# Dilated attention on quadrants of the array: 64 queries by 192 keys in place of 128 by 256

## The chip, the cores and the metric

The kernel runs on one core of a Trainium2 chip. A core has a matrix engine (PE, with its weight loads shown as PEld), a vector engine (DVE), a scalar engine (ACT), GpSimd (POOL) and a queue engine (SP) that issues most of the DMAs here. The metric is the device time of one execution in microseconds; the median of several runs is compared.

## The reference

Two layers of a decoder trunk over 1024 positions of width 1024, all in float32. The first layer mixes by dilated sliding-window attention, the second by a gated linear recurrence; each is followed by a squared-ReLU MLP. Only the attention is touched here:

```python
DILATED_PATTERNS = ((128, 1), (512, 4), (2048, 16))      # (window, dilation)
proj = (x @ w_in).reshape(B, S, N_GROUPS, 3, ATTN_HEADS, ATTN_HEAD_DIM)
for g, (window, dilation) in enumerate(DILATED_PATTERNS):
    q, k = rotary(proj[:, :, g, 0], pos), rotary(proj[:, :, g, 1], pos)
    o, lse = dilated_window_attention(q, k, proj[:, :, g, 2], window, dilation)
...
s = jnp.einsum('znqhe,znkhe->znhqk', qb, kk).astype(F32) * (E ** -0.5)
dist = qi + blk - kj
in_band = (dist >= 0) & (dist <= blk)
p = jnp.exp(s - m)
l = jnp.sum(p, axis=-1, keepdims=True)
o = jnp.einsum('znqhk,znkhe->znqhe', (p / l).astype(v.dtype), vv)
```

There are 16 heads of width 64. Each query sees itself and the 128 keys before it (128/1, 512/4) in its residue class, or 64 positions of its class at dilation 16 (a class has only 64). So in a block of 128 queries, query number i needs the keys i to i + 128 of the 256 keys of its own and the previous block: a band of 129.

## The kernel before

Everything is kept transposed: 128 partitions are the two heads of a pair (64 rows each), the free axis is the 1024 positions, regrouped by residue class. The queries, keys and values of a pair and a dilation (a *unit*; 8 pairs by 3 dilations, in the order 16, 4, 1) come out of a projection that is made by `product` (L787 to L832): 252 steps of 12 matmuls of 128 x 512 (L797 to L799). The attention of a unit is cut into pieces (`pieces`, L533), and the loop over the 252 products (L895) puts one list of pieces behind each product by a table (`fill`, with the offsets `OFFS`, `ROPES`, `STATS`, `MIX`). In that loop the order of PE and of DVE is fixed as written (`in_order`, L873); ACT and SP are ordered by the scheduler. The last two units (pair 7, dilations 4 and 1) go behind the loop and are spread over the first rows of the output projection, in the single-block form that `tail` returns (L663), with nothing fixed on PE.

For dilations 1 and 4 (g = 0 and 1) a unit has 8 blocks of 128 queries. A block *has a predecessor* (`has_prev`, L536) if it isn't the first of its class: 7 of 8 at dilation 1, 4 of 8 at dilation 4.

- `vtrans` (L539): 8 transposes of 128 x 128 turn vT into vn (keys on partitions), and ACT copies it out of PSUM in two halves (L546). vT is not used any more after that, and its slot of the pool `up` (49 slots of 4 KB per partition, for weights, activations and most else) comes free.
- `qk` (L549): per block and head one matmul with the 64 rows of that head, 128 queries as weights and 256 keys (128 without a predecessor) as moving columns, into the two banks `sb` (one for each head). DVE adds the mask and takes the row minimum (L572), ACT the exponential and the sum (L575). The result lies in a tile p as [head 0 | head 1], 256 columns each.
- `ptr` (L622): transposes p by 128 columns: four a block with a predecessor, two without (two such blocks share a tile), and ACT copies them to pts (L631).
- `pv` (L633): per block two key blocks by two heads, each a matmul with 128 keys on the rows, 64 columns of vn as weights and 128 queries moving, into the half of the bank `o` that belongs to the head. After four blocks ACT copies `o` to og (L650, L653).

Dilation 16 (`qk16`, `ptr16`, `pv16`, L578 to L620) already works on 64 x 64 quadrants: rows by head, columns by class.

SP's queue issues in one order: x operands (L449), weights (L460), the four DMAs that swap halves for the rotary (rot, L527), the softmax statistics (ml, L704 and L707) and weights for mixing the dilations (frow, L743), and for the output projection wor, onr and z (L1000, L1013, L1051).

Of the kernel before, what the change touches and what calls it, by code (L numbers as in the profile page):

```python
# [9 lines left out]
F32 = mybir.dt.float32  # L10
# [3 lines left out]
ALU = mybir.AluOpType  # L14
AX = mybir.AxisListType

P = 128
# [3 lines left out]
HD = 64  # L21
# [48 lines left out]
def trunk_kernel(  # L70
# [286 lines left out]
    def attention(pre, hc):  # L357
# [136 lines left out]
                v = nc.vector  # L494
                v.tensor_sub(H[n][:, R], lows.pop(n), H[n][:, L].bitcast(F32))  # L495

        mask = cp.tile([P, 320], F32, name="mask")
        sel = cp.tile([P, NG * P], F32R, name="bsel")
        frow = U("frow", F32R)
        mdram = dp.tile([NPAIR, NG, 2, 2, S], F32, name="mdram")  # L500
# [32 lines left out]
        def pieces(pr, g, qT, kT, vT, og, sS, tail):  # L533
            st = {}

            def has_prev(b):  # L536
                return (g == 0 and b > 0) or (g == 1 and b % 2 == 1)

            def vtrans():  # L539
                vn = U("vn")  # L540
                for j in range(2):
                    pt = bank("pt", "vpt")
                    for i in range(4):
                        b = j * 4 + i
                        nc.tensor.transpose(pt[:, i * P:(i + 1) * P], vT[:, b * P:(b + 1) * P], ident)
                    act(vn[:, j * 512:(j + 1) * 512], pt, AF.Copy)  # L546
                st["vn"] = vn

            def qk(*tiles):  # L549
                sb = [bank("s", "s") for _ in range(2)]  # L550
                at, c0 = {}, 0
                for b in sum(tiles, ()):
                    prev = has_prev(b)
                    n = 256 if prev else 128
                    k0 = (b - 1 if prev else b) * P
                    at[b] = slice(c0, c0 + n)
                    c0 += n
                    for h in range(2):
                        nc.tensor.matmul(sb[h][:, at[b]], qT[h * HD:(h + 1) * HD, b * P:(b + 1) * P],  # L559
                                         kT[h * HD:(h + 1) * HD, k0:k0 + n], start=True, stop=True,  # L560
                                         skip_group_check=True)
                for tile_ in tiles:
                    whole = wp.tile([P, 512], F32, name="p", tag="p")
                    st["p", tile_] = whole
                    for i, b in enumerate(tile_):
                        prev = has_prev(b)
                        n = 256 if prev else 128
                        m = mask[:, 0:256] if prev else mask[:, 128:256]
                        p = [whole[:, (2 * i + h) * n:(2 * i + h + 1) * n] for h in range(2)]
                        for h in range(2):  # L570
                            nm = sS[:, 0, h, b:b + 1]
                            nc.vector.tensor_tensor_reduce(p[h], sb[h][:, at[b]], m, -0.125, 3.0e38,  # L572
                                                           op0=ALU.add, op1=ALU.min, accum_out=nm)
                        for h in range(2):
                            act(p[h], p[h], AF.Exp, bias=sS[:, 0, h, b:b + 1], scale=-1.0,  # L575
                                accum_out=sS[:, 1, h, b:b + 1])

            def qk16(j):  # L578
                sb = [bank("s", "s") for _ in range(2)]
                whole = wp.tile([P, 512], F32, name="p", tag="p")  # L580
                blocks = [(b, cl, slice((b % 4 * 2 + cl) * 64, (b % 4 * 2 + cl) * 64 + 64))
                          for b in range(4 * j, 4 * j + 4) for cl in range(2)]
                for b, cl, c in blocks:
                    q = slice(b * P + cl * 64, b * P + cl * 64 + 64)
                    for h in range(2):
                        r = slice(h * HD, (h + 1) * HD)
                        nc.tensor.matmul(sb[cl][(h ^ cl) * HD:(h ^ cl) * HD + HD, b % 4 * 64:b % 4 * 64 + 64],
                                         qT[r, q], kT[r, q], start=True, stop=True, skip_group_check=True)
                for b, cl, c in blocks:
                    nc.vector.tensor_tensor_reduce(whole[:, c], sb[cl][:, b % 4 * 64:b % 4 * 64 + 64],  # L590
                                                   mask[:, 256:320], -0.125, 3.0e38, op0=ALU.add, op1=ALU.min,
                                                   accum_out=sS[:, 0, cl, b:b + 1])
                for b, cl, c in blocks:
                    act(whole[:, c], whole[:, c], AF.Exp, bias=sS[:, 0, cl, b:b + 1], scale=-1.0,
                        accum_out=sS[:, 1, cl, b:b + 1])
                st["p", j] = whole
# [25 lines left out]
            def ptr(tile_):  # L622
                pt = bank("pt", "ppt")
                pts = wp.tile([P, 512], F32, name="pts", tag="pts", bufs=4)
                p = st.pop(("p", tile_))
                n = len(tile_) * 2 * (2 if has_prev(tile_[0]) else 1)
                for i in range(n):
                    nc.tensor.transpose(pt[:, i * P:(i + 1) * P], p[:, i * P:(i + 1) * P], ident)  # L628
                for i, b in enumerate(tile_):
                    st["pt", b] = pts[:, i * 256:]  # L630
                act(pts[:, :n * P], pt[:, :n * P], AF.Copy)  # L631

            def pv(b):  # L633
                if b % 4 == 0:
                    st["o"] = bank("o", "o")
                o = st["o"]
                pts = st.pop(("pt", b))
                nb = 2 if has_prev(b) else 1
                for i in range(nb):
                    kb = b - nb + 1 + i  # L640
                    for h in range(2):
                        nc.tensor.matmul(o[h * HD:(h + 1) * HD, (b % 4) * P:(b % 4 + 1) * P],
                                         st["vn"][:, kb * P + h * HD:kb * P + (h + 1) * HD],
                                         pts[:, (h * nb + i) * P:(h * nb + i + 1) * P],
                                         start=i == 0, stop=i == nb - 1, skip_group_check=True)
                if b % 4 == 3:
                    hb = b // 4
                    d = DIL[g]
                    if d == 1:
                        act(og[:, hb * 512:(hb + 1) * 512], o, AF.Copy)  # L650
                    else:
                        r = d // 2
                        act(og.rearrange("p (n r) -> p r n", r=d)[:, hb * r:(hb + 1) * r, :],  # L653
                            o.rearrange("p (r n) -> p r n", r=r), AF.Copy)

            def qks(*tiles):
                return [lambda: qk(*tiles)]

            def run(f, bs):
                return [lambda b=b: f(b) for b in bs]  # L660

            one = [(b,) for b in range(8)]
            if tail:  # L663
                return [
                    qks(*one[0:2]) + [vtrans],
                    qks(*one[2:4]) + run(ptr, one[0:2]),
                    run(pv, (0, 1)) + qks(*one[4:6]) + run(ptr, one[2:4]),
                    run(pv, (2, 3)) + qks(*one[6:8]) + run(ptr, one[4:6]),
                    run(pv, (4, 5)) + run(ptr, one[6:8]),
                    run(pv, (6, 7)),  # L670
                ]
            first, second = run(pv, range(4)), run(pv, range(4, 8))
            if g == 2:
                return [run(qk16, (0,)) + [vtrans], run(qk16, (1,)) + run(ptr16, (0,)), run(ptr16, (1,)),
                        [pv16], [], []]
# [1244 lines left out]
def _constants():  # L1920
    import numpy as np

    f = np.float32
    half = HD // 2
    inv = (f(10000.0) ** (-np.arange(half, dtype=f) * f(2.0 / HD))).astype(f)
    ang = inv[:, None] * np.arange(S, dtype=f)[None, :]
    c, s = np.cos(ang).astype(f), np.sin(ang).astype(f)
    cos_t = np.concatenate([c, c, c, c], 0)
    sin_t = np.concatenate([-s, s, -s, s], 0)
    qi = np.arange(P)[:, None]  # L1930
    kj = np.arange(P)[None, :]
    neg = f(-1.0e30)
    prev = np.where(kj >= qi, f(0), neg)
    own = np.where(kj <= qi, f(0), neg)
    pk = np.where(kj[:, :64] <= qi % 64, f(0), neg)
    masks = np.concatenate([prev, own, pk], 1).astype(f)
    cm = ((kj >= qi) & (kj // CH == qi // CH)).astype(f)
    cmask = np.tile(cm, (1, 4))
    sm = np.ones((P, S), f)
    sm[:, ::CH] = 0.0  # L1940
    rows = np.arange(P)[:, None]
    bsel = np.concatenate([((rows // 4 == g) & (rows % 2 == np.arange(P)[None, :] // HD)).astype(f)
                           for g in range(NG)], 1)
    return {"cos_t": cos_t, "sin_t": sin_t, "masks": masks, "cmask": cmask, "smask": sm, "bsel": bsel}
# [49 lines left out]
```

## Time and profile before

| | us |
|---|---|
| median of 3 runs | 2746.34 (2744.36 to 2746.37) |
| the profiled execution | 2742.7 |
| its span in the profile | 2740.9 |
| mean granted clock of PE, share of full | 0.998 |
| matmul records of scores, values and transposes at dilations 1 and 4 | 1808 (512, 864, 432) |

The page lists engines with their busy time and share, groups of instructions by line with "out<-in", shape, count, busy time and the mean in ns of one, and what the engine waited for before them. A shape like 64*128 ahead of an operand's is that of the array: rows by columns used. Rows of a timeline begin with the start and the time to the modelled end of the last instruction of the row, both in us. Rows of a table by stage give the stage, its length, then busy time and instructions in it for PE, PEld, DVE, ACT and POOL. Rows "A <- B: t, n, m" say that A waited for B for t us in total, n times, at most m us.

### The profile page before, as it was taken

The numbers are of one execution on the slowest core, as the hardware profiler recorded it, in microseconds if no ns is written. First come the engines' busy times: TensorE is split into PE (matmuls) and PEld (weight loads), VectorE is DVE, ScalarE is ACT, GpSimd is POOL, SyncE is SP. The second block draws the span as 40 slices with busy tenths as digits, with TensorE's granted clock in tenths as the row PEclk, the third lists the DMA queues.
The fourth block names the chain that finished last, engine by engine and source line by source line (L and its number), as shares of the span: only waits on it lengthen the run. The fifth ranks groups of instructions, "written<-read, shape, count | busy, mean of one in ns | idle before, by whom it ended". The sixth has DMA issues, their size and how long they took to land.

```text
span 2740.9 us, 41042 instructions
## 1 busy us (share of the span) xinstructions
PE 2714.7 (99%) x14760; PEld 2218.5 (81%) x14760; DVE 2069.9 (76%) x3876; ACT 1402.9 (51%) x3043; POOL 68.9 (3%) x46
## 2 busy tenths in 40 slices
PE   9999999999999999999999999999999999999998
PEld 7788888888788777888888888888888888888887
DVE  8868887787887779776696787566578886778687
ACT  5555555555555546444554345555542544445443
POOL 0000000000000002000000000011100100000000
PEclk9999999999999999999999999999999999999999
DMA  8767666767767324554675752010242464485653
GB/s 301 262 210 228 195 209 190 235 193 225 217 208 243 109 98 156 192 193 151 205 266 167 237 169 93 31 59 35 74 127 100 154 226 162 152 297 181 220 179 127
DMA packets 204299, 485.03 MB, mean 177 GB/s; under 512 B 29248, under 2 KB 43072, under 8 KB 204096
## 3 DMA queue, kind: packets, MB, share of 16 engines
q1 hardware_dynamic: 203328, 482.16, 53.2%
q8 instruction: 116, 1.90, 0.3%
q14 instruction: 87, 0.71, 0.1%
q10 hardware_dynamic: 768, 0.26, 0.0%
HBM read 362.66 MB, written 94.11 MB: 167 GB/s over the span
## 4 chain that ended last, share of the span: by engine, by line
PE 90%; DVE 7%; ACT 2%; issue 1%; DMA 1%; SPq 0%; POOL 0%; DVEq 0%; ACTq 0%; POOLq 0%
PE pmm L797 7%; PE pmm L799 7%; PE pmm L798 7%; PE pup L1319 7%; PE pup L1317 7%; PE pup L1318 7%; PE pdy L1471 4%; PE pdy L1468 4%; PE pdy L1472 4%; PE pdx L1471 3%; PE pdx L1472 3%; PE pdx L1468 3%; PE pmm L192 3%; PE pmm L194 3%; PE pmm L193 3%; PE ppt L628 2%
## 5 line engine op out<-in xcount | busy, mean ns | idle before, releaser
L797 PE MATMUL pmm<-xh,H 128*128 128x512 f32 x1008 | 403.7, 400 | 1.9 <-ACT H L487 1.9
L799 PE MATMUL pmm<-xh,H 128*128 128x512 f32 x1008 | 394.6, 391 | 1.7 <-DVE H L495 1.6
L798 PE MATMUL pmm<-xl,H 128*128 128x512 f32 x1008 | 393.9, 391 | 0.7 <-DVE xl L158 0.7
L799 PEld LDWEIGHTS pmm<-xh,H 128*128 128x128 f32 x1008 | 189.6, 188 | 44.1 <-DVE H L495 3.3
L797 PEld LDWEIGHTS pmm<-xh,H 128*128 128x128 f32 x1008 | 189.9, 188 | 40.8 <-ACT H L487 3.0
L798 PEld LDWEIGHTS pmm<-xl,H 128*128 128x128 f32 x1008 | 190.0, 189 | 38.1 <-DVE xl L158 1.5
L1468 PE MATMUL pdy<-dT,dS 128*128 128x512 f32 x512 | 199.2, 389 | 0.0
L1471 PE MATMUL pdy<-dT,dS 128*128 128x512 f32 x512 | 199.2, 389 | 0.0
L1472 PE MATMUL pdy<-dT,dS 128*128 128x512 f32 x512 | 199.2, 389 | 0.0
L575 ACT ACTIVATE p<-p,stats 128x256 f32<-128x256 f32 (+1 forms) x256 | 118.3, 465 | 72.8 <-DVE stats L572 72.1
L157 ACT ACTIVATE dS<-dr 128x512 fp32r<-128x512 f32 x192 | 119.3, 622 | 68.5 <-PE pdy L1472 35.5
L192 PE MATMUL pmm<-f0nh,wh 128*128 128x512 f32 x384 | 153.2, 399 | 0.0
L194 PE MATMUL pmm<-f0nh,wl 128*128 128x512 f32 x384 | 149.8, 390 | 0.0
L193 PE MATMUL pmm<-f0nl,wh 128*128 128x512 f32 x384 | 149.7, 390 | 0.0
L158 DVE TENSOR_TENSOR dS<-dr,dS 128x512 fp32r<-128x512 f32 x192 | 131.4, 685 | 9.2 <-ACT dS L157 9.2
L572 DVE CUSTOM_DVE_ANT_0 p<-s,mask 128x256 f32<-128x256 f32 (+1 forms) x256 | 82.7, 380 | 58.4 <-PE s L559 49.0
L157 ACT ACTIVATE dT<-hold 128x512 fp32r<-128x512 f32 x128 | 80.1, 626 | 80.7 <-DVE hold L1447 34.0
L1278 ACT ACTIVATE H<-wc 128x512 fp32r<-128x512 f32 x128 | 77.2, 625 | 77.2 <-DVE wc L1271 47.9
L1468 PEld LDWEIGHTS pdy<-dT,dS 128*128 128x128 f32 x512 | 96.1, 188 | 20.1
L1472 PEld LDWEIGHTS pdy<-dT,dS 128*128 128x128 f32 x512 | 96.1, 188 | 19.9
L1471 PEld LDWEIGHTS pdy<-dT,dS 128*128 128x128 f32 x512 | 96.1, 188 | 19.9
L487 ACT ACTIVATE H<-wc 128x512 fp32r<-128x512 f32 x108 | 66.6, 630 | 70.4 <-DVE wc L479 53.8
(424 smaller groups left out, 6860.4 us busy)
## 6 DMA issues: line engine op xcount, KB each, us to landing
xh<-xtd SPq DMA_DIRECT2D x110, 512.0 KB
xl<-xtd SPq DMA_DIRECT2D x110, 512.0 KB
dr<-hd SPq DMA_DIRECT2D x192, 256.0 KB
dr<-in_w_down_dram SPq DMA_DIRECT2D x128, 256.0 KB
rot<-e SPq DMA_DIRECT2D x192, 128.0 KB
wa<-in_w_up_dram SPq DMA_DIRECT2D x48, 512.0 KB
wb<-in_w_attn_dram SPq DMA_DIRECT2D x36, 512.0 KB
wa<-in_w_attn_dram SPq DMA_DIRECT2D x33, 512.0 KB
```

What stands on the lines that cost most here:

```text
L157: act(hi, raw, AF.Copy)
L192: nc.tensor.matmul(o, wh[:, k], xs.h(k), start=k == 0, stop=False)
L193: nc.tensor.matmul(o, wh[:, k], xs.l(k), start=False, stop=False)
L194: nc.tensor.matmul(o, wl[:, k], xs.h(k), start=False, stop=k == NK - 1)
L797: nc.tensor.matmul(o, wh, hi[k // 2][:, c], start=begin and k == 0, stop=False, skip_group_check=True)
L798: nc.tensor.matmul(o, wh, lo[k // 2][:, c], start=False, stop=False, skip_group_check=True)
L799: nc.tensor.matmul(o, wl, hi[k // 2][:, c], start=False, stop=end and k == 3, skip_group_check=True)
L1317: nc.tensor.matmul(o, wh, xf.h(b, k), start=begin and k == 0, stop=False, skip_group_check=True)
L1318: nc.tensor.matmul(o, wh, xf.l(b, k), start=False, stop=False, skip_group_check=True)
L1468: nc.tensor.matmul(o[q], h, T_[:, L], start=begin, stop=False, skip_group_check=True)
L1471: nc.tensor.matmul(o[q], h, T_[:, R], start=False, stop=False, skip_group_check=True)
L1472: nc.tensor.matmul(o[q], l, T_[:, L], start=False, stop=end, skip_group_check=True)
```

## The change

The 128 queries of a block with a predecessor are taken in two halves a = 0, 1 of 64. Half a needs the keys 64 a to 64 a + 191 of the 256, so 192 columns stand in p for each head, not 256. The scores become four matmuls (half by head), each on its own 64 x 64 quadrant; blocks without a predecessor are split the same way with 128 keys each. The tile p of a block is [head 0, 192 | head 1, 192] and has three transposes; the middle one holds the last 64 keys of head 0 on its upper 64 partitions and the first 64 of head 1 on its lower ones. Where the 128 keys on the partitions don't begin at a block, values are needed that are shifted by 64: three DMAs on SP write them from vn over vT, which lives on until the last value product. Per half and head there is now one product over 128 keys (`first`) and one over the other 64 (`rest_`), both with 64 moving columns. `pv` takes all blocks of a call together and makes all of `first` before all of `rest_`. The mask has a band for 192 columns.

```diff
-        mask = cp.tile([P, 320], F32, name="mask")
+        mask = cp.tile([P, 384], F32, name="mask")
...
                 st["vn"] = vn
+                if g < 2:
+                    nc.sync.dma_start(vT[0:HD, :], vn[HD:P, :])
+                    nc.sync.dma_start(vT[HD:P, 0:7 * P], vn[0:HD, P:])
+                    nc.sync.dma_start(vT[HD:P, 7 * P:], vn[0:HD, 0:P])
...
-                    n = 256 if prev else 128
-                    k0 = (b - 1 if prev else b) * P
+                    n = 192 if prev else 128
                     at[b] = slice(c0, c0 + n)
                     c0 += n
-                    for h in range(2):
-                        nc.tensor.matmul(sb[h][:, at[b]], qT[h * HD:(h + 1) * HD, b * P:(b + 1) * P],
-                                         kT[h * HD:(h + 1) * HD, k0:k0 + n], start=True, stop=True,
-                                         skip_group_check=True)
+                    for a in range(2):
+                        k0 = (b - 1) * P + a * 64 if prev else b * P
+                        for h in range(2):
+                            r = slice(h * HD, (h + 1) * HD)
+                            nc.tensor.matmul(sb[h][a * 64:a * 64 + 64, at[b]],
+                                             qT[r, b * P + a * 64:b * P + a * 64 + 64], kT[r, k0:k0 + n],
+                                             start=True, stop=True, skip_group_check=True)
...
-                n = len(tile_) * 2 * (2 if has_prev(tile_[0]) else 1)
+                n = 3 if has_prev(tile_[0]) else 2 * len(tile_)
...
-                for i in range(nb):
-                    kb = b - nb + 1 + i
-                    for h in range(2):
-                        nc.tensor.matmul(o[h * HD:(h + 1) * HD, (b % 4) * P:(b % 4 + 1) * P],
-                                         st["vn"][:, kb * P + h * HD:kb * P + (h + 1) * HD],
-                                         pts[:, (h * nb + i) * P:(h * nb + i + 1) * P],
-                                         start=i == 0, stop=i == nb - 1, skip_group_check=True)
+                vn = st["vn"], vT
+                first, rest_ = [], []
+                for b in bs:
+                    pts = st.pop(("pt", b))
+                    for a, h in ((a, h) for a in range(2) for h in range(2)):
+                        f = slice(h * HD, (h + 1) * HD)
...
+                        if not has_prev(b):
+                            if a == 0:
+                                first.append((o[f, b % 4 * P:(b % 4 + 1) * P], v(0, b), pts[:, h * P:(h + 1) * P]))
+                            continue
+                        to = o[f, b % 4 * P + a * 64:b % 4 * P + a * 64 + 64]
+                        whole = v(a, b - 1) if h == 0 else v(1 - a, b - 1 + a)
+                        part = v(a, b, f) if h == 0 else v(1 - a, b - 2 + a, f)
+                        first.append((to, whole, pts[:, h * 256 + a * 64:h * 256 + a * 64 + 64]))
+                        rest_.append((to, part, pts[f, P + a * 64:P + a * 64 + 64]))
+                for n, (to, w, m) in enumerate(first):
+                    nc.tensor.matmul(to, w, m, start=bs[0] % 4 == 0 and n < 2, stop=False, skip_group_check=True)
+                for to, w, m in rest_:
+                    nc.tensor.matmul(to, w, m, start=False, stop=True, skip_group_check=True)
...
-            first, second = run(pv, range(4)), run(pv, range(4, 8))
+            first, second = [lambda: pv(0, 1, 2, 3)], [lambda: pv(4, 5, 6, 7)]
...
+    band = np.arange(192)[None, :] - qi % 64
+    prev = np.where((band >= 0) & (band <= P), f(0), neg)
```

The function `v(shift, t, r)` picks 64 columns of a head from vn (shift 0) or from the shifted copy in vT (shift 1), block t modulo 8, rows r. In the tail, `pv` is called for two blocks at a time, as in `[lambda: pv(0, 1)]`.

More of the change, by code (lines that the diff above doesn't have):

```diff
@@ L566, in qk @@
                         prev = has_prev(b)
-                        n = 256 if prev else 128
-                        m = mask[:, 0:256] if prev else mask[:, 128:256]
+                        n = 192 if prev else 128
+                        m = mask[:, 0:192] if prev else mask[:, 192:320]
                         p = [whole[:, (2 * i + h) * n:(2 * i + h + 1) * n] for h in range(2)]
@@ L590, in qk16 @@
                     nc.vector.tensor_tensor_reduce(whole[:, c], sb[cl][:, b % 4 * 64:b % 4 * 64 + 64],
-                                                   mask[:, 256:320], -0.125, 3.0e38, op0=ALU.add, op1=ALU.min,
+                                                   mask[:, 320:384], -0.125, 3.0e38, op0=ALU.add, op1=ALU.min,
                                                    accum_out=sS[:, 0, cl, b:b + 1])
@@ L631, in ptr, with pv, v @@
                 act(pts[:, :n * P], pt[:, :n * P], AF.Copy)
-            def pv(b):
-                if b % 4 == 0:
+            def pv(*bs):
+                if bs[0] % 4 == 0:
                     st["o"] = bank("o", "o")
                 o = st["o"]
-                pts = st.pop(("pt", b))
-                nb = 2 if has_prev(b) else 1
-                for i in range(nb):
-                    kb = b - nb + 1 + i
-                    for h in range(2):
-                        nc.tensor.matmul(o[h * HD:(h + 1) * HD, (b % 4) * P:(b % 4 + 1) * P],
-                                         st["vn"][:, kb * P + h * HD:kb * P + (h + 1) * HD],
-                                         pts[:, (h * nb + i) * P:(h * nb + i + 1) * P],
-                                         start=i == 0, stop=i == nb - 1, skip_group_check=True)
+                vn = st["vn"], vT
[4 more added lines that the diff above has]
+                        f = slice(h * HD, (h + 1) * HD)
+                        def v(shift, t, r=slice(0, P)):
+                            return vn[shift][r, t % 8 * P + f.start:t % 8 * P + f.stop]
+                        if not has_prev(b):
[11 more added lines that the diff above has]
+                    nc.tensor.matmul(to, w, m, start=False, stop=True, skip_group_check=True)
+                b = bs[-1]
                 if b % 4 == 3:
@@ L666, in pieces @@
                     qks(*one[2:4]) + run(ptr, one[0:2]),
[L667 to L670, printed above, removed]
+                    [lambda: pv(0, 1)] + qks(*one[4:6]) + run(ptr, one[2:4]),
+                    [lambda: pv(2, 3)] + qks(*one[6:8]) + run(ptr, one[4:6]),
+                    [lambda: pv(4, 5)] + run(ptr, one[6:8]),
+                    [lambda: pv(6, 7)],
                 ]
-            first, second = run(pv, range(4)), run(pv, range(4, 8))
+            first, second = [lambda: pv(0, 1, 2, 3)], [lambda: pv(4, 5, 6, 7)]
             if g == 2:
@@ L1932, in _constants @@
     neg = f(-1.0e30)
-    prev = np.where(kj >= qi, f(0), neg)
     own = np.where(kj <= qi, f(0), neg)
+    band = np.arange(192)[None, :] - qi % 64
+    prev = np.where((band >= 0) & (band <= P), f(0), neg)
     pk = np.where(kj[:, :64] <= qi % 64, f(0), neg)
```

## The prediction

> **What bounds the kernel.** I read the page first, then who waits for whom on PE, then a table by stage, then the groups by line and shape.
>
> ```profile
> span 2740.9 us, 41042 instructions
> PE 2714.7 (99%) x14760; PEld 2218.5 (81%) x14760; DVE 2069.9 (76%) x3876; ACT 1402.9 (51%) x3043; POOL 68.9 (3%) x46
> PE pmm L205 <- DVE wol L158: 1.9, 2, 1.1
> 85.00:940.00 855.00, 851.71 (x5736) 688.16 (x5736) 674.69 (x1504) 479.60 (x1312) 0.96 (x1) 1.00 0.67 210
> 940.00:1060.00 120.00, 114.13 (x623) 86.92 (x622) 91.78 (x216) 68.39 (x193) 2.10 (x2) 1.00 0.32 111
> ```
>
> PE is busy 99% of the span, and its worst releaser (the view is sorted, this is its first row) costs 1.9 us; no DMA is among its releasers. The table's columns are PE, PEld, DVE, ACT, POOL, granted clock, DMA share, GB/s. In attention (85 to 940 us) PE works 851.71 of 855 us at full clock, DVE 674.69, ACT 479.60, the DMA engines 0.67. So a microsecond that PE no longer needs there leaves the span, and what DVE and ACT save (narrower reductions, exponentials and copies) is worth nothing: I cost it at zero. After 940, PE idles 5.9 of 120 us: there the end of attention is partly a chain through DVE, ACT and SP, and I count less.
>
> ```profile
> L628 PE MATMUL ppt<-ident,p 128*128 128x128 f32 x432 | 60.3, 279 | 0.5 <-ACT vn L546 0.4
> L642 PE MATMUL o<-pts,vn 128*64 128x128 f32 x864 | 56.8, 277 | 0.0
> L559 PE MATMUL s<-kT,qT 64*128 64x256 f32 x352 | 52.5, 399 | 0.0
> L559 PE MATMUL s<-kT,qT 64*128 64x128 f32 x160 | 14.9, 296 | 0.6 <-DVE kT L531 0.5
> ```
>
> That is 184.5 us of PE that the change touches. Counts: per pair there are 11 blocks with a predecessor (7 at dilation 1, 4 at dilation 4) and 5 without, over 8 pairs 88 and 40. Scores take 2 matmuls a block, so 176 and 80, and the rows count 352 and 160: **one matmul leaves two records**; a transpose leaves one (54 a pair, 432).
>
> **PE's prices, start to start.** The modelled ends are not usable, the starts are. Rows of the timeline:
>
> ```profile
> 84.68 0.39 PE L799 MATMUL pmm<-xh,H 128*128 128x512 f32 x1
> 85.00 0.69 PE L587 MATMUL s<-kT,qT 64*64 64x64 f32 x32
> 85.62 1.09 PE L545 MATMUL vpt<-ident,vT 128*128 128x128 f32 x8
> 86.47 0.47 PE L797 MATMUL pmm<-xh,H 128*128 128x512 f32 x1
> ...
> 105.74 1.16 PE L615 MATMUL o<-pts,vn 64*64 64x64 f32 x64
> 106.84 0.50 PE L797 MATMUL pmm<-xh,H 128*128 128x512 f32 x1
> ...
> 117.55 0.39 PE L798 MATMUL pmm<-xl,H 128*128 128x512 f32 x1
> 117.78 0.39 PE L799 MATMUL pmm<-xh,H 128*128 128x512 f32 x1
> 118.10 1.16 PE L559 MATMUL s<-kT,qT 64*128 64x128 f32 x16
> 119.19 1.09 PE L545 MATMUL vpt<-ident,vT 128*128 128x128 f32 x8
> ...
> 125.68 1.14 PE L559 MATMUL s<-kT,qT 64*128 64x256 f32 x8
> 126.75 1.09 PE L628 MATMUL ppt<-ident,p 128*128 128x128 f32 x8
> ...
> 140.80 1.53 PE L642 MATMUL o<-pts,vn 128*64 128x128 f32 x24
> 142.27 1.09 PE L628 MATMUL ppt<-ident,p 128*128 128x128 f32 x8
> ...
> 196.58 1.97 PE L642 MATMUL o<-pts,vn 128*64 128x128 f32 x32
> 198.47 0.69 PE L587 MATMUL s<-kT,qT 64*64 64x64 f32 x32
> 199.10 1.09 PE L545 MATMUL vpt<-ident,vT 128*128 128x128 f32 x8
> ```
>
> - Quadrants (64*64), 64 columns: 32 records 0.62, 64 records 1.10. A matmul on another quadrant runs beside its neighbours, four abreast, so these are 8 and 16 steps: 0.06 a step, and 0.14 for entering and leaving the shape.
> - Column halves (128*64), 128 columns, two abreast: 24 records 1.47, 32 records 1.89, so 12 and 16 steps of 0.105 to 0.109 and about 0.15 around them. I use 0.109.
> - Row halves (64*128), two abreast: 16 records of 128 columns 1.09 (8 steps), 8 records of 256 columns 1.07 (4 steps). With 0.109 for 128 columns, 0.22 lies around them and 256 columns take 0.2125. By the line through both, **192 columns take 0.161**.
> - A transpose: 8 in 0.85 (85.62 to 86.47), 0.106 each.
> - The entry is seen alone too: L798 to L799 is 0.23, L799 to L559 0.32, L799 to L587 0.32.
>
> **The change part by part**, for one of the seven pairs inside the product loop.
>
> (a) *Scores.* Two matmuls of 256 columns on row halves become four of 192 on the four quadrants: still two steps a block, 0.161 for 0.2125, and 0.15 around a call for 0.22. Nothing shows four abreast at 192 columns; the bounds are L587 (four abreast, as here) and L559 (two abreast), and I take L587, whose shape it is. Five calls with two such blocks: 1.07 becomes 0.15 + 4 x 0.161 = 0.79, saving 0.27 each. The call of blocks 0 and 1: 0.22 + 0.22 + 0.43 = 0.86 becomes 0.15 + 0.22 + 0.32 = 0.69, saving 0.17. The call of four first blocks: 1.09 becomes 1.02, saving 0.07. Sum **-1.6**.
>
> (b) *Transposes.* Four become three on 11 blocks: 11 x 0.106, **-1.2**.
>
> (c) *Values.* Per block with a predecessor four matmuls of 128 columns (4 steps of 0.109, 0.44) become four whole ones of 64 columns on column halves (4 steps) and four part ones of 64 columns on two opposite quadrants (two abreast, 4 steps): 8 x 0.06 = 0.48. Nothing is saved; a change of shape, about 0.15, is added between the two lists of each call. Dilation 4, twice: 1.47 becomes 0.15 + 0.44 + 0.48 + 0.15 + 0.48 = 1.70, +0.23. Dilation 1, first half (28 records, 14 steps, 1.68): 0.15 + 0.22 + 0.72 + 0.15 + 0.72 = 1.96, +0.28. Second half: 1.89 becomes 0.15 + 0.96 + 0.15 + 0.96 = 2.22, +0.33. Together +1.07. But in three of the four calls scores come next on PE (rows 196.58 to 198.47 show one), and part products and scores are then both 64*64: that entry of 0.15 goes if the shape alone decides, -0.45. No row shows two 64*64 lines in a row; bounds are 0 and -0.45, and I take -0.45, because 32 and 64 records within L587 and L615 run on without it. Net **+0.6**.
> The Trainium skill, "TensorEngine Tiling (Array Packing)", section "Tiling Modes", says that changing the mode drains the array and changing the tile alone does not; the 0.32 for 0.23 agrees with the first half, and by the second half the free entry is right.
>
> (d) *Three DMAs for each of 16 units*, 512 KB each, on SP's queue: they wait for the second vn copy, and the slot of vT stays taken until the last value product. Rows by SP, ACT, DVE and PE for the tightest kind of unit, and SP's longest kind of wait for slots:
>
> ```profile
> 234.38 0.87 PE L545 MATMUL vpt<-ident,vT 128*128 128x128 f32 x6
> ...
> 241.57 1.06 ACT L546 ACTIVATE vn<-vpt 128x512 f32<-128x512 f32 x2
> ...
> 241.62 2.47 SPq L527 DMA_DIRECT2D rot<-e  x4
> ...
> 249.41 1.23 DVE L530 TENSOR_TENSOR rot<-rot,sinT 128x1024 f32<-128x1024 f32 x1 [1.31 <-DMA rot<-e]
> ...
> 257.01 1.53 PE L642 MATMUL o<-pts,vn 128*64 128x128 f32 x24
> SPq L449 <- PE pmm L799: 121.3, 53, 6.5
> SPq L743 <- DVE H L495: 38.0, 8, 10.5
> ```
>
> vn is whole at 242.6, the products want the shifted copy at 257.0: 14.4 us. The nearest transfer, rot's four DMAs of 128 KB, was issued at 241.62 and waited for until 249.41, 7.8 us. So the copy lands some 6 us early, and I cost it at **0**; the cover is the slots of products between. If SP stands behind a wait (10.5 us at worst in the L743 row) the cover is gone, and PE, whose order is fixed, holds everything behind the value product: products, and DVE behind them. Behind the new wait on SP stand rot, x and weight loads. 8.4 MB more at 210 GB/s is 40 us of a queue with a third of 855 us free. The wider mask (384 columns for 320) is one load at the start, long before its use. The slot costs the x loads (L449) some lead: they already wait for PE to free slots. Bounds: 0, and up to 6.5 us for a unit.
>
> **Sum.** -1.6 - 1.2 + 0.6 = -2.2 a pair, seven pairs **-15.4**. The last pair lies after 917 us in single-block pieces among output-projection rows, with more changes of shape and six new DMAs on SP ahead of frow and ml: between -2 and +3, I take **-0.5**. Together -16 on the profiled execution, 2742.7 (span 2740.9 and 1.8 around it). That run stands 3.6 under the median of the three, 2746.34, which is what will be compared: 2746 - 16 = **2730**.
>
> **Rivals.**
> 1. *Part products take turns* (slower). Heads 0 and 1 use different row halves and write the same bank o. If they can't do so at once, 4 steps of the part list become 8: 88 x 4 x 0.06 = +21, net +5, **2751**. It decides from three of the four. Against: L587 writes each of its two banks from both row halves and still runs four abreast. 5%. The Trainium skill, same page, "Restrictions and Gotchas", says that different row tiles cannot access the same bank simultaneously; the L587 rows speak against that for disjoint partitions.
> 2. *Narrow whole products cost what wide ones do*, 0.109 instead of 0.06 (a bound by weight loading on 128*64): 88 x 4 x 0.05 = +18, **2748**, no change. For: no row has 128*64 at 64 columns. Against: the quadrants load as many weight columns in each step of 0.06. 5%.
> 3. *The shifted copy or the loads come late.* Each us that PE waits per unit costs 16; from 1.0 us per unit the gain is gone. Likelier a few units or the last pair: +4 to +14, **2738**, in the extreme 2750. For: L743 and L449 rows; against: 6 us of spare. 12%.
> 4. *Quadrants do not overlap at 192 columns*: four steps for two, 88 x 2 x 0.161 = +28, **2758**. 2%.
>
> **Chances and range.** The forecast has 76%: its own bounds are -20 (last pair at -2, finer steps, 2 us between runs) and -8 (no free entry, 7 x 0.45 = +3; last pair +3; 2 between runs), 2726 to 2738. The range 2724 to 2744 takes in the milder half of rival 3 and leaves out the rest. 0.2% is 5.5 us, about what a measurement of this kernel can tell from none. Faster: 76 and 7 of rival 3, 83%. Same: 3 of rival 2, 3 of rival 3, 6%. Slower: 11%.
>
> **What would show it.** Scores of two 192-column blocks in 0.65 to 0.8 us start to start; six transposes, not eight, in a step with two such blocks, and 48 us of them in all where the row has 60.3; a value call of four blocks at about 2.1 to 2.2 with the part records two abreast at 0.06; no 0.09 extra from part products to scores; no new row with a DMA among PE's releasers; PE idle in attention still some 3 us. I am wrong if PE waits on vT, if the part list takes twice as long, or if the attention stage shortens by 15 us and the stage after 940 gives it back.

## The result, and the profile after

The changed kernel takes **2766.56 us** (median of 4 runs, 2764.17 to 2772.61) against 2746.36 before (2744.36 to 2746.99): a ratio of **1.0080, 95% interval 1.0067 to 1.0092**. The forecast was 2730, in a range of 2724 to 2744; it was wrong in sign. The profiled execution took 2764.17.

From the page of the changed kernel:

```profile
span 2762.3 us, 43402 instructions
PE 2708.0 (98%) x15888; PEld 2210.6 (80%) x15888; DVE 2057.7 (74%) x3876; ACT 1386.9 (50%) x3043; POOL 68.9 (2%) x46
```

From its table by stage, attention (columns as in the prediction):

```profile
85.00:940.00 855.00, 828.35 (x6649) 667.18 (x6648) 647.67 (x1478) 460.59 (x1305) 0.95 (x1) 0.99 0.69 218
```

PE has less to do over the whole span (2708.0 us where it was 2714.7), and the span is 21.4 us longer. In the 855 us of attention, where PE worked 851.71, it now works 828.35: it stands still for 26.7 us in place of 3.3. So the arithmetic became cheaper and PE waits. For whom, by the view of waits, PE's first row, then the rows of DVE and SP that matter:

```profile
PE pmm L820 <- DVE H L495: 21.5, 10, 3.3
...
DVE rot L530 <- DMA rot<-e: 51.3, 11, 7.5
...
SPq L549 <- ACT H L487: 46.9, 14, 14.7
```

The products (L820) wait ten times, 21.5 us in all, for their low weights H, which DVE makes (L495); before, the first row of this view had 1.9 us. DVE waits 51.3 us for rot, up to 7.5 us at once. SP stands 46.9 us at L549, the first of the three new DMAs, until ScalarE has copied vn out (the row names H, which ScalarE begins at that moment). These are three links of one chain. The chain of what ended last, from 249 to 267 us of the changed kernel, with start and length, shows them in order:

```profile
249.69 0.96 ACT vn L546 x2
...
251.25 0.59 SPq L550
...
251.88 0.63 SPq L551
...
252.56 0.94 SPq L449
...
254.04 0.56 SPq L527
...
256.17 7.14 DMA rot<-e
...
263.40 1.24 DVE rot L530
...
265.80 0.70 DVE H L495
...
266.54 0.50 PE pmm L820
```

Read it downwards: vn is evicted; SP, which had stood at L549, issues the three copies, then two x loads, and only then rot (L527, from 254.04); the last rot piece is 7.14 us in flight; DVE, whose order is fixed, has stood at L530 since 255.9 and does the rotary and then the weights; the product starts. In the kernel before the four rot DMAs were issued at 241.62, beside the vn copy at 241.57. Here the vn copy starts at 249.59 and rot 4.4 us after it. The row of DVE in the prediction, `[1.31 <-DMA rot<-e]`, is the same instruction before: it waited even then, so there rot had no time to lose. It was issued 6.5 us before DVE came to it (241.62 to 248.10) and is now issued 1.8 us before (254.04 to 255.87).

DVE waits ten times for rot between 85 and 940 us, 50.0 us in all, and seven of these waits are over 6 us. Three are of this kind, 21.2 us together. The other four, 26.8 us together, are at places where rot did have time before: it was issued 11 to 13.5 us ahead of DVE, which waited 0.5 us at most. Now it is issued 3.6 us ahead (at 408.08 for a DVE that comes at 411.70, for one).

What a stall of PE costs beyond itself is in PE's timeline of the changed kernel:

```profile
266.54 0.50 PE L820 MATMUL pmm<-xh,H 128*128 128x512 f32 x1 [3.11 <-DVE H L495]
266.87 0.39 PE L818 MATMUL pmm<-xh,H 128*128 128x512 f32 x1
267.10 0.39 PE L819 MATMUL pmm<-xl,H 128*128 128x512 f32 x1
...
268.06 0.63 PE L819 MATMUL pmm<-xl,H 128*128 128x512 f32 x1
268.49 0.63 PE L820 MATMUL pmm<-xh,H 128*128 128x512 f32 x1
```

and in its table by stage:

```profile
262.00:276.00 14.00, 10.89 (x77) 8.37 (x76) 10.80 (x21) 3.97 (x13) 0.00 (x0) 0.88 0.89 281
```

After 3.11 us idle the matmuls of the products start 0.23 to 0.33 apart, and from 267.63 they are 0.43 apart. The granted clock in this stage of 14 us is 0.88: 0.12 x 14 = 1.7 us are lost, half of 3.4. The changed kernel has four such stretches between products 21 and 246, after four of its six idle times of 2.9 to 3.3 us; the kernel before has none there. The Trainium skill, "TensorE: Matmul & The Clock Gate", Part 1, says that the clock is halved after an idle window of about 3.4 us and is full again after a busy window of that length. The trace agrees on the length of the stretch, 3.41 us, and not on the idle time, which was shorter each time (2.87 to 3.21).

The account for products 21 to 246, from the first matmul of the one to that of the other (seven pairs): 821.2 us before, 839.3 after, **+18.1**. PE's idle gaps there go from 1.1 to 25.4, +24.3. Taken from start to start, less these gaps, the matmuls of attention take 172.6 for 188.1, -15.5, and those of the products 641.3 for 632.0, +9.3. The half clock is 4 x 1.7 = 6.8 of the 9.3; the other 2.5 stay open.

### The profile page after: what moved, and what is told of

It reads as the page before. It is cut to its first block, busy times and chain, and to the rows that moved or that the text cites. A ratio compares the mean times of both kernels' runs of the same rounds, so it can differ in the third digit from the quotient of the medians.

```text
span 2762.3 us, 43402 instructions
## 1 busy us (share of the span) xinstructions
PE 2708.0 (98%) x15888; PEld 2210.6 (80%) x15888; DVE 2057.7 (74%) x3876; ACT 1386.9 (50%) x3043; POOL 68.9 (2%) x46
## 4 chain that ended last, share of the span: by engine, by line
PE 86%; DVE 7%; ACT 3%; DMA 2%; issue 1%; SPq 1%; POOL 0%; DVEq 0%; ACTq 0%; POOLq 0%
PE pup L1340 7%; PE pup L1338 7%; PE pup L1339 7%; PE pmm L820 6%; PE pmm L818 6%; PE pmm L819 6%; PE pdy L1492 4%; PE pdy L1489 4%; PE pdy L1493 4%; PE pdx L1492 3%; PE pdx L1493 3%; PE pdx L1489 3%; PE pmm L192 3%; PE pmm L194 3%; PE pmm L193 3%; PE pmm L206 2%
## 5 line engine op out<-in xcount | busy, mean ns | idle before, releaser
L820 PE MATMUL pmm<-xh,H 128*128 128x512 f32 x1008 | 398.2, 395 | 21.7 <-DVE H L495 21.5
L819 PE MATMUL pmm<-xl,H 128*128 128x512 f32 x1008 | 396.4, 393 | 1.8 <-DMA xl<-xtd 1.1
L820 PEld LDWEIGHTS pmm<-xh,H 128*128 128x128 f32 x1008 | 191.0, 190 | 68.5 <-DVE H L495 27.4
L819 PEld LDWEIGHTS pmm<-xl,H 128*128 128x128 f32 x1008 | 191.5, 190 | 40.5 <-DMA xl<-xtd 2.2
L581 ACT ACTIVATE p<-p,stats 128x192 f32<-128x192 f32 (+1 forms) x256 | 108.7, 428 | 62.5 <-DVE stats L578 62.3
L578 DVE CUSTOM_DVE_ANT_0 p<-s,mask 128x192 f32<-128x192 f32 (+1 forms) x256 | 70.7, 334 | 44.7 <-PE s L565 34.3
```

Source lines behind the costliest of these rows:

```text
L819: nc.tensor.matmul(o, wh, lo[k // 2][:, c], start=False, stop=False, skip_group_check=True)
L820: nc.tensor.matmul(o, wl, hi[k // 2][:, c], start=False, stop=end and k == 3, skip_group_check=True)
```

## The experiments

Theories before the first runs: A, the copies' wait on SP holds rot and with it DVE and PE; B, the copies' transfers do it; C, vT's slot, which is held longer, does it. Medians and intervals are against the kernel before on the same chip (2745.9 to 2746.2).

**1. No copies.** The value products read what stands in vT.

```diff
-                if g < 2:
-                    nc.sync.dma_start(vT[0:HD, :], vn[HD:P, :])
-                    nc.sync.dma_start(vT[HD:P, 0:7 * P], vn[0:HD, P:])
-                    nc.sync.dma_start(vT[HD:P, 7 * P:], vn[0:HD, 0:P])
```

> The changed kernel without the three DMAs that shift the values: the value products read vT as it is, so the attention of dilations 1 and 4 is computed with unshifted values where shifted ones are due. PE's work, DVE's and ACT's and the life of vT's slot stay. Theory A (order on SP: the copies stand on SP's queue until vn is there, rot stands behind them, DVE waits for rot and PE for DVE's low weights) and theory B (the bytes of the copies delay rot's bytes on the shared DMA engines) both expect 2727 to 2735 us, PE waits as in the kernel before (some 17 us in all), no half-clock stretch in the attention loop. Theory C (vT's slot, kept until the last value product, starves the loads) expects it to stay above 2755.

Measured: 2726.16 us, ratio 0.9928 (0.9913 to 0.9943). Its table by stage:

```profile
85.00:940.00 855.00, 850.03 (x6887) 686.80 (x6885) 674.65 (x1549) 473.99 (x1354) 0.95 (x1) 1.00 0.67 211
```

and in the view of waits:

```profile
DVE rot L530 <- DMA rot<-e: 9.9, 6, 2.8
```

DVE's wait for rot before:

```profile
DVE rot L530 <- DMA rot<-e: 9.5, 6, 3.0
```

PE is full again and the wait for rot is what it was before. Products 21 to 246 take 806.2 us, 15.0 less than before. So the three DMAs cost 40 us, the arithmetic brings its gain, and C is out: the slot is held here as long.

**2. The same copies issued by ScalarE, 3. copies of a few bytes, 4. the kernel before with copies that nobody reads.**

```diff
-                    nc.sync.dma_start(vT[0:HD, :], vn[HD:P, :])
+                    nc.scalar.dma_start(vT[0:HD, :], vn[HD:P, :])
```

```diff
-                    nc.sync.dma_start(vT[0:HD, :], vn[HD:P, :])
-                    nc.sync.dma_start(vT[HD:P, 0:7 * P], vn[0:HD, P:])
-                    nc.sync.dma_start(vT[HD:P, 7 * P:], vn[0:HD, 0:P])
+                    nc.sync.dma_start(vT[0:HD, 0:8], vn[HD:P, 1016:1024])
+                    nc.sync.dma_start(vT[HD:P, 0:8], vn[0:HD, 1016:1024])
+                    nc.sync.dma_start(vT[HD:P, 8:16], vn[0:HD, 1016:1024])
```

(2 alike for all three DMAs; 4 adds the three lines of 1 to the kernel before.)

> The same three DMAs issued from ACT's queue, right behind the ACT copy that writes vn; the same bytes, nothing on SP. Theory A expects 2728 to 2738 us, with DVE's wait for rot back to 10 to 20 us from 51. Theory B expects 2755 to 2767, with rot as late as in the changed kernel.

> The three DMAs stay on SP with the same waits, but move 8 columns (64 x 32 bytes) each in place of 512 KB together; the values read are therefore not the shifted ones. Theory A expects most of the loss to stay: 2750 to 2767 us. Theory B expects 2728 to 2738.

> The kernel before, with nothing changed but the three DMAs added on SP (they write vT, which nobody reads any more; the output stays right). Theories A and B expect 2772 to 2786 us (the loss of the changed kernel against its 16 us of saved PE work), with DVE waiting some 50 us for rot and PE waits of 25 us more than in the kernel before. Theory C expects at most 2752, since vT's slot comes free as soon as the copy has landed.

Measured: 2753.31 (ratio 1.0031, 1.0019 to 1.0043); 2746.68 (1.0003, 0.9994 to 1.0013); 2772.15 (1.0097, 1.0082 to 1.0113). First, waits of DVE and SP in 2 (copies by ScalarE):

```profile
DVE rot L530 <- DMA rot<-e: 35.4, 12, 9.2
...
SPq L725 <- DMA vT<-vn: 27.7, 15, 5.1
SPq L527 <- DMA vT<-vn: 25.7, 6, 6.3
```

and a row of SP's timeline there:

```profile
236.37 9.85 SPq L725 DMA_DIRECT2D ml<-mdram  x8
```

SP waits 27.7 us at L725 and 25.7 us at L527 for the landing of the copies, though ml and rot have nothing to do with vT, and the copies are on another queue. The eight ml issues take 9.85 us where the kernel before needed 2.81. In the trace of this run the DMAs of SP and ScalarE use the same eight completion semaphores (100 to 107), and a DMA waits until the one before it on its semaphore has landed: the ml issue on 107 stands until 242.55, for the copy that ScalarE issued on 107 at 240.76. So moving a DMA to ScalarE's queue doesn't take it out of SP's way.

The same waits in 3 (few bytes, still on SP):

```profile
DVE rot L530 <- DMA rot<-e: 35.8, 10, 6.7
SPq L549 <- ACT H L487: 73.4, 14, 14.1
```

Without the bytes, run 3 still takes 20.5 us more than no copies: about half of the 40. So neither A nor B has run 2 or run 3 in its range; in front of rot the wait and the bytes both count. DVE's three long waits where rot was 6.5 us ahead come to 18.7 us in run 3 (21.2 in the changed kernel), the other four to 13.2 (26.8).

In 4 the copies cost 26 us with the arithmetic of the kernel before, so most of the loss doesn't need the new shapes. In products 21 to 246 they cost 26.7 us there (847.9 for 821.2) and 33.1 in the changed kernel (839.3 for 806.2); where the other 6.4 come from is open. Open too: in each of 2, 3 and 4 the scheduler also ordered ScalarE's instructions in another way than in the same kernel without copies, so a part could be ScalarE's.

**5. DVE's use of rot up to two products later; 6. copies behind rot; 7. both; 8. control: the kernel before with the later use.** If DVE at rot is the link, either edit should remove it.

```diff
-ROPES = ((-5, -3, -3, -1, 1, 2), (5, 7, 7, 9, 11, 11))
+ROPES = ((-5, -1, -1, -1, 3, 3), (5, 9, 9, 9, 13, 13))
```

and in 6, the copies in a piece of their own one step later, each behind the last four rot DMAs on SP:

```diff
+            def shifted():
+                vn = st["vn"]
+                nc.sync.dma_start(vT[0:HD, :], vn[HD:P, :])
+                behind(latest(), last_rot[-4:])
...
+            return [qks(*one[0:2]) + [vtrans], qks(*one[2:4]) + run(ptr, one[0:2]) + [shifted],
...
+                if g < 2 and a and not last:
+                    at(base + 17, p[1].pop())
```

> The changed kernel with its three copies where they are; only DVE's use of rot (the products with cos and sin and what leads to the low and high weights of the next pair) stands up to two products later in DVE's order. Theory A (the only harm is DVE standing at a late rot, 51.3 us of it in the changed kernel, and TensorE standing behind DVE's weights): the gaps of TensorE in products 21 to 246 fall from 25.4 us to under 8, the half-clock stretches are gone, 2726 to 2738 us. Theory B (x and weight loads behind the copies, or the copies themselves, are late for TensorE as well): gaps stay over 13 us, over 2750 us. Theory E (the weights become late by my own move, whatever rot does): DVE's wait for rot falls under 15 us but TensorE's waits on the low and high weights stay over 15 us; 2745 to 2770 us.

> The changed kernel with the three copies of a unit issued later: in a later piece of the unit, and on SP behind the four rot DMAs that the changed kernel has waiting behind them. Everything else as in the changed kernel. Theory A (what costs is the order on SP: rot behind the wait for vn): DVE's wait for rot falls from 51.3 us to about the 10 us of the kernel before, the gaps of TensorE in products 21 to 246 to under 5 us, 2726 to 2738 us. Theory B (the transfers themselves hurt, by their packets or by the ring of eight semaphores that every later DMA goes through): part of the wait stays, at x, the weight loads or ml; 2745 to 2765 us. Theory F (the copies now land too late for the products with the shifted values): TensorE waits on vT for over 10 us in all, over 2750 us.

> The two edits together: copies behind rot on SP, and DVE's use of rot up to two products later. Theory A: no better than the better of the two by more than 4 us, 2724 to 2736 us, since each alone removes the one link. Theory B: 2740 to 2760 us. If the ring of eight semaphores still holds rot after the move, this is the one that gains most over the copies behind rot alone (5 to 15 us).

> Control: the kernel before, with DVE's use of rot up to two products later and nothing else. If the later use is only a cover for a late rot, it is worth nothing where rot is early: 2742 to 2750 us. If the later use is a gain by itself, under 2740 us, and then the gain of the late use in the changed kernel doesn't show that rot was the link. Over 2752 us: the later use makes the weights late by itself.

Measured: 5, 2776.63 (1.0113, 1.0098 to 1.0128); 6, 2747.26 (1.0005, 0.9996 to 1.0015); 7, 2780.2 (1.0127, 1.0110 to 1.0143); 8, 2778.58 (1.0118, 1.0101 to 1.0135). The control settles 5 and 7: the later use costs 33 us where rot is early. None of 5, 6 and 7 came into the range of theory A. Waits of DVE and PE in 5, from 85 to 940 us:

```profile
DVE rot L530 <- DMA rot<-e: 2.4, 3, 1.0
...
PE s L565 <- DVE kT L531: 8.1, 3, 2.7
PE pmm L820 <- DVE H L495: 7.0, 7, 1.1
```

DVE no longer waits for rot, but now the scores wait for kT and the products for H. DVE's fixed order has no slack in that direction either, so 5 and 7 don't test theory A; they were badly chosen. Run 6 gained 19 us, about half of what was expected; DVE's wait for rot fell to 8.5 us between 85 and 940 us (6.5 before). PE's first two waits in it:

```profile
PE mpt L717 <- ACT og L679: 6.7, 4, 1.8
PE mpt L720 <- ACT og L682: 6.4, 3, 2.1
```

and the timeline of ScalarE and PE at one of them:

```profile
264.69 0.60 ACT L857 ACTIVATE e<-pmm 128x512 f32<-128x512 f32 x1 [2.60 <-PE pmm L828]
...
265.66 1.08 ACT L682 ACTIVATE og<-o 128x512 f32<-128x512 f32 x1
...
266.79 0.48 PE L720 MATMUL mpt<-ident,stats 128*128 128x128 f32 x1 [2.14 <-ACT og L682]
```

The stall at H has gone. Instead PE stands seven times, 13.1 us, at the transpose of the statistics, which needs the bank `o` (mpt lies there in the loop); og, which empties it, stands on ScalarE behind a copy (L857) that waits 2.60 us for the next product. In the run without copies og stood ahead of that copy. ScalarE's order isn't fixed in the loop (but for products 30 to 33), and the scheduler made another one when the DMAs were added.

**9. Copies issued by POOL.** In the product loop PE, DVE, ScalarE and SP then keep the order of run 1, as the traces of both show.

```diff
-                    nc.sync.dma_start(vT[0:HD, :], vn[HD:P, :])
+                    nc.gpsimd.dma_start(vT[0:HD, :], vn[HD:P, :])
```

(alike for all three)

> The changed kernel with its three copies of a unit issued by POOL instead of SP: same bytes, same place in the program, same arithmetic. The orders of the instructions on TensorE, VectorE, ScalarE and SP are then, through the product loop, those of the kernel without the copies (2726 us); only POOL, busy in one instruction between 85 and 940 us, stands and waits for vn. Theory A (the cost is the copies' place in front of other work: SP's order, and ScalarE's order that the scheduler made with it, not the transfers): 2724 to 2734 us, gaps of TensorE in products 21 to 246 under 4 us, DVE's wait for rot about 10 us; this would beat the kernel before by 12 to 22 us. Theory B (the transfers themselves cost, by their packets beside the other queues' or because they share the ring of semaphores): 2742 to 2765 us, with waits at rot, x or ml. Theory F (issued by POOL the copies land late for the values): TensorE waits on vT for over 10 us in all, 2740 us or more.

Measured: **2732.41 us, ratio 0.9950 (0.9936 to 0.9964)**. The table by stage:

```profile
85.00:940.00 855.00, 846.31 (x6807) 683.81 (x6799) 670.60 (x1524) 468.53 (x1333) 25.79 (x49) 1.00 0.70 220
```

DVE's wait for rot from 85 to 940 us (6.8 in run 1, 50.0 in the changed kernel):

```profile
DVE rot L530 <- DMA rot<-e: 16.7, 7, 5.1
```

POOL's timeline has the first of three copies,

```profile
239.73 0.52 POOL L551 DMA_DIRECT2D vT<-vn  x1 [76.57 <-ACT vn L546]
```

and the chain the last rot piece of that time:

```profile
240.79 9.38 DMA rot<-e
```

The same bytes at the same place in the program, and 34 us less than with SP: in theory A's range, with somewhat more waiting than A expected (PE's gaps in products 21 to 246 are 5.9). POOL may stand for 76 us, since nothing but the copies is behind it. The transfers aren't free: the last rot piece, issued beside the copies, is 9.38 us in flight (6.8 for the last piece of the same rot in run 1), and products 21 to 246 take 812.7 us, 6.5 more than with no copies. The Trainium skill, "Trainium Kernel Development and Optimization", Key Constraints, says that all queues run on the same 16 DMA engines and that issuing from several saves only issue time. The 9.38 us fit the first half; the 34 us don't fit the second: here the other queue took a *wait* out of SP's way. ScalarE's order changed too between the two; run 10 below has it as it is here, with the copies on SP, and takes 32.6 us longer.

**10. and 11. ScalarE's order pinned.** The order of run 1 (1011 instructions, ACTS gives how far each is moved) is imposed on the changed kernel (10) and on run 6 (11).

```diff
+        row = [i for i in list(nc.cur_bb.bb.instructions)[n_act:] if i.engine == mybir.EngineType.Activation]
+        row = [row[k + ord(c) - ord("A") - 9] for k, c in enumerate(ACTS)]
+        for i, j in zip(row, row[1:]):
+            tc.add_manual_dep(j, i.name, mybir.DependencyInfo(
+                mybir.DependencyClass.NoSync, mybir.DependencyReason.DATA), reason="acts")
```

> The changed kernel, copies on SP as they are, with ScalarE's order in the product loop pinned to the order that the kernel without the copies has (in the changed kernel the scheduler puts about a seventh of ScalarE's rows elsewhere). SP's order is untouched, copies in front of rot. Theory S (what costs is SP: rot behind the wait for vn, and the copies' landing in the ring): most of the 34 us that the changed kernel stands above the copies-on-POOL version stay, 2752 to 2768 us, DVE's wait for rot over 30 us. Theory R (ScalarE's reordering is most of it: og evictions, low weights and the vn eviction come later than they could): 2730 to 2742 us, TensorE's gaps in products 21 to 246 under 10 us.

> The copies on SP behind rot and in a later piece (2747 us), with ScalarE's order pinned as in the kernel without the copies. In the version without the pin TensorE stood seven times for 1.4 to 2.1 us at the transposes of the statistics, which waited for an og eviction that stood behind a later product's copy on ScalarE. Theory R' (that reordering is its whole loss): those waits go, 2726 to 2736 us. Theory S' (the copies on SP still hold x, ml or rot through order or ring): the waits turn up elsewhere, 2740 to 2755 us.

Measured: 10, 2764.98 (1.0067, 1.0052 to 1.0082); 11, **2730.51 (0.9944, 0.9928 to 0.9961)**. Of 10, the row of the table by stage, and under it DVE's wait for rot in the same stretch:

```profile
85.00:940.00 855.00, 828.52 (x6623) 668.22 (x6622) 650.67 (x1485) 462.87 (x1310) 0.95 (x1) 0.99 0.69 218
DVE rot L543 <- DMA rot<-e: 49.7, 10, 8.2
```

The same two rows of 11:

```profile
85.00:940.00 855.00, 849.69 (x6854) 686.17 (x6852) 672.95 (x1545) 473.93 (x1354) 0.95 (x1) 1.00 0.71 220
DVE rot L546 <- DMA rot<-e: 8.9, 5, 3.2
```

| median, us | ScalarE as scheduled | ScalarE as in run 1 |
|---|---|---|
| copies ahead of rot on SP | 2766.56 (the change) | 2764.98 (10) |
| copies behind rot, a piece later | 2747.26 (6) | 2730.51 (11) |
| copies issued by POOL | | 2732.41 (9) |

With the copies ahead of rot, ScalarE's order makes no difference that these runs can tell (1.6 us); that the stall at H covers it is likely, but not shown. With rot first, 19 us come back, and ScalarE's order is then worth 17 more. Runs 10 and 11 have ScalarE in one order and differ only in the place of the copies: 34.5 us. (Whether it is being behind rot or being a piece later that helps was not tried apart.) Products 21 to 246 take 806.3 us in run 11 and 806.2 in run 1: inside the loop, the three DMAs cost **nothing** that can be told once they stand in the right place. The 4 us that are left lie outside the loop. Runs 9 and 11 both beat the kernel before, by 14 and 15 us.

So the price was the place in SP's queue. Ahead of rot the copies cost the loop 33.1 us, behind it the same bytes cost 0.1. Of the 33.1, 17.8 are there with hardly any bytes (run 3, 824.0 for 806.2): the traffic counts where it stands in front of a transfer that the wait has already made late.

## Why the prediction was wrong

- **What bounds the kernel: right.** PE was full, and what PE saved came out of the span one for one when nothing else moved (run 1: 806.2 for 821.2 in the loop, -15.0; forecast -15.4).
- **(a) and (b) right.** Scores of two blocks and transposes in PE's timeline of the changed kernel:

```profile
126.23 0.88 PE L565 MATMUL s<-kT,qT 64*64 64x192 f32 x16
127.04 1.09 PE L634 MATMUL ppt<-ident,p 128*128 128x128 f32 x8
...
272.25 0.87 PE L634 MATMUL ppt<-ident,p 128*128 128x128 f32 x6
272.88 0.48 PE L818 MATMUL pmm<-xh,H 128*128 128x512 f32 x1
```

  0.81 start to start where 0.79 was forecast, and 0.63 for six transposes (0.64). Rival 4 falls.
- **(c) right.** A value call of dilation 4 takes 1.67 (1.70 forecast). The chain has the two lists of one,

```profile
161.88 1.05 PE o L663 x24
162.93 0.55 PE o L665 x13
```

  and the timeline the starts within a part list:

```profile
271.63 0.27 PE L665 MATMUL o<-pts,vn 64*64 64x64 f32 x1
271.64 0.27 PE L665 MATMUL o<-pts,vT 64*64 64x64 f32 x1
...
272.10 0.22 PE L665 MATMUL o<-pts,vn 64*64 64x64 f32 x1
```

  Part products start in pairs 0.01 apart, and the 16 of them take 0.62 (271.63 to the transposes at 272.25): two abreast into one bank, so rival 1 falls, and with it, for tiles on disjoint partitions, the rule of the Trainium skill that the prediction weighed there. The list of whole products, 24 records, takes 1.05 (1.07 forecast), so rival 2 falls. Where scores follow the part list, their records come between the last part records (163.47 and 163.53 in the same chain): entering costs nothing, as taken. Summed from start to start over the loop, run 1 against the kernel before, a pair saves 1.5 in scores and 1.2 in transposes and pays 0.5 in values; the forecast was 1.6, 1.2 and 0.6. Together that is 2.24 (forecast 2.2).
- **(d) is the step that failed**: "So the copy lands some 6 us early, and I cost it at 0". I asked when the copy is needed and not what it pushes back. Both halves of the answer stood in the prediction: "Behind the new wait on SP stand rot, x and weight loads", and the row of L530 with its 1.31 us of waiting for rot, which I read as the time of a transfer and not as a transfer *without slack*. That row stands for three of the seven long waits; at the other four rot had a lead, and the copies took 7 to 10 us of it. From there the chain is fixed: rot late, DVE's order, H, PE. It costs the loop 33.1 us (839.3 less 806.2), 4.7 us a pair, against a gain of 2.2. With this step put right, in run 11, the kernel takes 2730.51 us, where 2730 was forecast, and the loop gains 14.9 of the 15.4, so the sum holds there. That the totals agree to 0.5 us is partly luck, as the last pair shows.
- **Rival 3 named the case with a wrong size**: 2738, at most 2750. It summed the waits of value products for vT and of x loads for slots. The first never came: no row of PE names vT<-vn. Of the second, 1.1 us came (L819 for xl). What came instead were waits for H, and half clock after stalls of about 3 us, which no rival had.
- **The last pair** was forecast at -0.5. From product 251 to the first transpose of the norm behind the output projection (L253) it took 112.5 us before, 108.9 without copies (-3.6), 111.4 in run 11 (-1.1), 113.0 as changed (+0.5): the gain there is larger than forecast, and the copies take it back.

## What to carry to other kernels

A DMA that waits for a late producer is costed at the head of its queue: list what is issued behind it, and look up for each how far ahead of its consumer it is issued and whether that consumer already waits for it. One that waits has no slack, and the whole delay goes to it and to all that stands behind it in a fixed order; but a lead of 11 us was used up here as well. Put such a DMA behind the transfers that have no slack, or on a queue where nothing follows. And where a scheduler orders an engine, compare that engine's order before and after an edit elsewhere: here that alone was worth 17 us.

## What the runs showed of the hardware and was not expected

- Four of six stalls of 2.9 to 3.3 us in the changed kernel are followed by 3.41 us at half clock, 1.7 us lost: such a stall costs nearly 5 then. Shorter ones can do it too: two of the three of 2.14 us in run 6, and one of 1.81 us in run 9.
- Queues of different engines aren't independent in this program: SP waited 27.7 us at ml for copies that ScalarE had issued (run 2), because their DMAs share eight completion semaphores. No SP row in run 9 waits for the copies that POOL issued.
- Half a megabyte of copies beside rot lengthens the flight of rot: its last piece took 9.38 us in run 9 (6.8 in run 1) and 6.5 us of loop time went with it; issued behind rot the same copies cost the loop 0.1 us (run 11).
